# A DoRA linear layer on one core: the last three blocks loaded in 2 MB pieces behind two chunks of short rows, five chunks of short-row stores, earlier queued stores, and ScalarE for the first rounding

## The chip, the cores and the metric

One core of a Trainium2 chip. The metric is the device time of one execution in microseconds (us), median of several runs. Every timed run also carries the span that its own trace shows, about 1.3 us less than the time.

## The reference

The weights are small; the work is a product of 32768 rows by 256 with a 256 by 256 matrix. Input and output are 33.6 MB each.

```python
# x: (16, 2048, 256) float32; W: (256, 256); lora_A: (256, 16); lora_B: (16, 256); m: (256,)
W_adapted = W + scale * (lora_A @ lora_B)
W_norm = np.sqrt(np.sum(W_adapted ** 2, axis=0, keepdims=True) + 1e-8)
W_final = W_adapted / W_norm * m
y = x.reshape(-1, 256) @ W_final
```

## The kernel before

x is cut into 8 blocks of 4 MB. A block has 8 chunks of 512 KB; in SBUF a partition holds 32 rows of x per block, 32 KB that are also contiguous in HBM. Five blocks are held in SBUF at a time, so blocks 5 to 7 reuse the room of blocks 0 to 2, and can be loaded only once those are stored. y is written over x in the same buffer.

Two chunks make a pair. GpSimd (POOL) rounds a pair to bf16, TensorE turns it (transposes, two bf16 values at a time seen as one float32), VectorE copies it out of PSUM, TensorE multiplies it by w_final, ScalarE copies the two products from PSUM over x. Loads go through SyncE's queue, stores through ScalarE's.

```python
loads = [(0, 2), (2, 2), (4, CH - 4)] + units[1 : XBUFS - 1]      # (first chunk, chunks)
loads += [((XBUFS - 1) * CH, CH - 3)]
loads += [(XBUFS * CH - 3 + c, 1) for c in range(3)] + units[XBUFS:]
...
stores = [(b * CH, CH, 19 + b) for b in range(F - 1)]             # (first, chunks, issued after chunk)
stores += [(G - CH, CH // 2, 24), (G - CH // 2, CH // 2, 24)]
FIRST = len(stores)
stores += [(G + c, 1, G + 3) for c in range(4)]
stores += [(G + 4, CH - 4, 47)]
stores += [(b * CH, CH, max(47, (b + 1) * CH - 1)) for b in range(F + 1, NBLK - 1)]
stores += [(g0, cnt, g0 + cnt - 1) for g0, cnt in units[-2:]]
...
# POOL waits at pair 15 until the third store has landed (a rest of some 25 us)
if p == REST:
    nc.gpsimd.wait_ge(sem(f"store{HALF}"), 16)
```

The three one-chunk loads and the four one-chunk stores have rows of 4 KB per partition where a whole block has 32 KB.

## Time and profile before

| | before |
|---|---|
| median time, first three runs | 163.13 us (163.13 to 163.31) |
| span in the profile | 161.3 us |
| DMA engines: first packet to last packet | 2.0 to 160.8 us |
| PE, ACT, POOL, DVE busy | 61, 40, 39, 29% |
| mean rate | 418 GB/s |

The lines that matter most are shown in the prediction below. Two more, from the timeline of the kernel before near its start (columns: start us, length us, engine, line, operation, what it writes and reads, count): the products that make w_final, and the first transposes whose data come from block 1.

```profile
13.55 2.45 DVE L236 TENSOR_TENSOR w_final<-wam,rnorm 128x256 bf16<-128x256 f32 x2
...
27.09 1.04 PE L304 MATMUL xt_ps<-identity,xb 128*128 128x128 f32 x8
```

And this is the DMA view of the stretch from 160.0 to 163.5 us, beyond the point where 15 of the 16 engines are done (packets, MB, share of 16 engines):

```profile
q10 hardware_dynamic: 2, 0.02, 1.1%
```

One data packet of 16 KB and its completion packet: a single DMA engine works there, and the kernel waits for it.

### The profile page before, as it was taken

The page shows a single profiled execution, that of the slowest core. Times are in us where ns is not written, and L with a number is a line of the kernel's source. Part 1 is how long each engine was busy: PE and PEld are TensorE (multiplying, and loading weights), DVE is VectorE, ACT ScalarE, POOL GpSimd, SP SyncE. Part 2 cuts the span into 40 slices and gives each one's busy share as a digit, 9 for nine tenths or more (in the row PEclk, how much of TensorE's full clock was granted, in tenths as well). Part 3 has the DMA queues.
Part 4 walks back from the last instruction along what each step waited for, and adds up shares of the span by engine and source line. Part 5 has one row for each costly group of instructions (what it writes and reads, how often), then busy time and mean ns, then how long its engine had stood idle before and what let it go on. Part 6 is the DMA issues. An engine that isn't in the chain of part 4 may idle for free. (4 is left out here: it accounts for less than half of the span.)

```text
span 161.3 us, 2012 instructions
## 1 busy us (share of the span) xinstructions
PE 98.1 (61%) x786; PEld 85.6 (53%) x786; DVE 46.6 (29%) x44; ACT 64.1 (40%) x67; POOL 62.9 (39%) x39
## 2 busy tenths in 40 slices
PE   0490899999997920000799949999999980000000
PEld 0260789999996710000689937999799970000000
DVE  0539533535443500000224413445344500000000
ACT  3010068686776370000057643686767681000000
POOL 1174327868684000002938066497667400000000
PEclk9999999999999985555569995999999996555555
DMA  5999999999899999899999999999999999999994
GB/s 163 429 453 459 390 512 398 390 512 398 374 487 439 390 463 456 363 419 422 400 434 424 437 455 422 396 453 431 412 487 398 422 479 398 408 496 398 398 439 211
DMA packets 4357, 67.42 MB, mean 418 GB/s; under 512 B 626, under 2 KB 643, under 8 KB 1667
## 3 DMA queue, kind: packets, MB, share of 16 engines
q1 hardware_dynamic: 2160, 33.82, 49.2%
q10 hardware_dynamic: 2194, 33.59, 48.9%
q14 instruction: 3, 0.02, 0.0%
HBM read 33.85 MB, written 33.55 MB: 418 GB/s over the span
## 5 line engine op out<-in xcount | busy, mean ns | idle before, releaser
L258 ACT COPY x_sb<-y_ps 128x1024 f32<-128x1024 f32 x64 | 62.2, 1015 | 61.5 <-PE y_ps L318 60.2
L199 POOL CAST xb<-x_sb 128x2048 bf16<-128x2048 f32 x32 | 60.4, 1895 | 62.8 <-DMA out_dram<-x_sb 24.7
L318 PE MATMUL y_ps<-w_final,xt 128*128 128x256 bf16 x512 | 66.5, 286 | 2.5 <-PEq L293 2.5
L240 DVE COPY xt<-xt_ps 128x1024 f32<-128x1024 f32 x32 | 39.2, 1224 | 74.3 <-PE xt_ps L304 74.3
L318 PEld LDWEIGHTS y_ps<-w_final,xt 128*128 128x128 bf16 x512 | 52.3, 103 | 10.9 <-issue 3.2
L304 PE MATMUL xt_ps<-identity,xb 128*128 128x128 f32 x264 | 37.2, 288 | 25.7 <-PEq L293 25.7
L304 PEld LDWEIGHTS xt_ps<-identity,xb 128*128 128x128 f32 x264 | 32.3, 150 | 27.7 <-issue 27.2
L274 PE MATMUL y_ps<-identity,a_nat 128*16 128x128 f32 x2 | 0.6, 396 | 4.1 <-DMA a_nat<-in_lora_A_dram 4.1
L285 PE MATMUL y_ps<-sq,ones 128*128 128x256 f32 x4 | 2.1, 675 | 1.6 <-DVE sq L225 1.6
L250 ACT ACTIVATE norm<-y_ps,eps_col 128x256 f32<-128x256 f32 x1 | 0.5, 473 | 5.6 <-PE y_ps L285 5.6
L236 DVE TENSOR_TENSOR w_final<-wam,rnorm 128x256 bf16<-128x256 f32 x2 | 2.5, 1266 | 0.0
L285 PEld LDWEIGHTS y_ps<-sq,ones 128*128 128x128 f32 x4 | 1.2, 326 | 2.3 <-DVE sq L225 2.1
L274 PEld LDWEIGHTS y_ps<-identity,a_nat 128*16 128x16 f32 x2 | 0.1, 88 | 4.1 <-issue 4.1
L248 ACT ACT_TABLE_LOAD x1 | 1.3, 1283 | 2.4 <-issue 2.4
L205 POOL MEMSET xb<- 128x2048 bf16 x1 | 1.8, 1804 | 0.7 <-PE xt_ps L304 0.7
L233 DVE RECIPROCAL rnorm<-norm 128x256 f32<-128x256 f32 x1 | 1.7, 1747 | 0.0
L227 DVE COPY m_all<-y_ps 128x256 f32<-128x256 f32 x1 | 0.4, 424 | 3.3 <-PE y_ps L290 3.3
L290 PE MATMUL y_ps<-m_row,ones 1*128 1x256 f32 x2 | 1.2, 710 | 0.0
L216 DVE CAST b_bf<-b_nat 16x256 bf16<-16x256 f32 x1 | 0.3, 280 | 3.2 <-DMA b_nat<-in_lora_B_dram 3.2
L221 DVE SCALAR_TENSOR_TENSOR wa<-y_ps,w_nat 128x512 f32<-128x512 f32 x1 | 0.7, 692 | 0.8 <-PE y_ps L278 0.8
L278 PE MATMUL y_ps<-b_bf,aT 16*128 16x256 bf16 x2 | 0.6, 402 | 0.5 <-DVE aT L218 0.5
L290 PEld LDWEIGHTS y_ps<-m_row,ones 1*128 1x128 f32 x2 | 0.5, 308 | 0.7 <-issue 0.7
(13 smaller groups left out, 3.3 us busy)
## 6 DMA issues: line engine op xcount, KB each, us to landing
x_sb<-in_x_dram SPq DMA_DIRECT2D x5, 4096.0 KB, 28.7
out_dram<-x_sb ACTq DMA_DIRECT2D x5, 4096.0 KB, 20.9
out_dram<-x_sb ACTq DMA_DIRECT2D x5, 2048.0 KB, 26.7
x_sb<-in_x_dram SPq DMA_DIRECT2D x3, 2048.0 KB, 33.4
x_sb<-in_x_dram SPq DMA_DIRECT2D x1, 2560.0 KB, 44.7
x_sb<-in_x_dram SPq DMA_DIRECT2D x2, 1024.0 KB, 6.0
out_dram<-x_sb ACTq DMA_DIRECT2D x4, 512.0 KB, 43.8
x_sb<-in_x_dram SPq DMA_DIRECT2D x3, 512.0 KB, 19.5
```

Of the source, the lines that this page charges most:

```text
L199: nc.gpsimd.tensor_copy(out=xb_bufs[p % NXB][:], in_=x_bufs[b % XBUFS][:, 2 * c * J : 2 * (c + 1) * J, :],).then_inc(sem("rounded"), 1)
L205: nc.gpsimd.memset(xb_bufs[NPR % NXB][:], 0.0).then_inc(sem("rounded"), 1)
L221: nc.vector.scalar_tensor_tensor(out=wa[:], in0=ab_ps, scalar=float(scale), in1=w_nat[:], op0=ALU.mult, op1=ALU.add).then_inc(dv, 1)
L233: nc.vector.reciprocal(out=rnorm[:], in_=norm[:]).then_inc(dv, 1)
L236: i = nc.vector.tensor_mul(out=w_final[:, t], in0=wam[:, t], in1=rnorm[:])
L240: nc.vector.tensor_copy(out=xt_bufs[p % NXT][:].rearrange("p r t -> p (r t)").bitcast(FP32), in_=xt_ps[p % 2][:],).then_inc(sem("copied"), 1)
L248: nc.scalar.activation(out=warm[:], in_=eps_col[:], func=AF.Sqrt)
L258: nc.scalar.copy(out=x_bufs[b % XBUFS][:, c * J : (c + 1) * J, :], in_=y_ps[g % 2][:]).then_inc(sem("room"), 1)
L285: i = nc.tensor.matmul(n2_ps, ones[:], sq[:, t, :], start=(t == 0), stop=(t == KC - 1))
L290: nc.tensor.matmul(mb_ps, ones[0:1, :], m_row[:], start=True, stop=True).then_inc(pe, 1)
L304: i = nc.tensor.transpose(xt_ps[p % 2][:, j * P : (j + 1) * P], xb_bufs[p % NXB][:, j, :].bitcast(FP32), identity[:],)
L318: i = nc.tensor.matmul(y_ps[h][:, j, :], xt_bufs[p % NXT][:, r : r + P, t], w_final[:, t, :], start=(t == 0 and (j % (J // 2)) == 0), stop ...
```

## The change

The intent is to keep both queues fed with better proportions. As the prediction reads from the trace, the two queues take turns on a DMA engine, one packet each, and a packet is one row; so short rows hold one queue back without stopping it. The change makes only two chunks of loads short (not three), follows them at once by blocks 5 to 7 in halves with waits of their own, makes five chunks of stores short (not four), queues blocks 3 and 4 for storing from chunk 44 on, and shortens the start by having ScalarE round the first pair.

```diff
-    loads = [(0, 2), (2, 2), (4, CH - 4)] + units[1 : XBUFS - 1]
-    loads += [((XBUFS - 1) * CH, CH - 3)]
-    loads += [(XBUFS * CH - 3 + c, 1) for c in range(3)] + units[XBUFS:]
+    loads = [(0, 2, 2 * J), (2, 2, 2 * J), (4, 4, 4 * J)]         # third number: rows of x (1 KB each) in one packet
+    loads += [(b * CH, CH, CH * J) for b in range(1, XBUFS - 1)]
+    loads += [(H - CH, 6, 6 * J), (H - 2, 2, J)]
+    loads += [(g0, 4, 4 * J) for g0 in range(H, NCH, 4)]
-    stores += [(G - CH, CH // 2, 24), (G - CH // 2, CH // 2, 24)]
+    stores += [(G - CH, 3, 3 * J, G), (G - 5, 5, 5 * J, G)]
-    stores += [(G + c, 1, G + 3) for c in range(4)]
-    stores += [(G + 4, CH - 4, 47)]
-    stores += [(b * CH, CH, max(47, (b + 1) * CH - 1)) for b in range(F + 1, NBLK - 1)]
+    stores += [(G, 4, J, G + 3), (G + 4, 1, J, G + 4)]
+    stores += [(G + 5, CH - 5, (CH - 5) * J, 44), (G + CH, CH, CH * J, 44)]
+    stores += [(b * CH, CH, CH * J, (b + 1) * CH - 1) for b in range(F + 2, NBLK - 1)]
...
-        if loads[n][0] == XBUFS * CH:            # block 5: waits for stores 0, 1 and 2
+        if loads[n][0] == H + CH:                # block 6: waits for store 1
+            wait_store(nc.sync, 1)
+        if loads[n][0] == H + 2 * CH:            # block 7: waits for stores 2 and 3
...
-    for p in range(NPR):
+    for p in range(1, NPR):
...
+        if p == 1:
+            nc.gpsimd.wait_ge(sem("dve"), 6)
+        if p == 2:
+            nc.gpsimd.wait_ge(sem("dve"), 8)     # w_final is done
...
+    wait_load(nc.scalar, 0)
+    nc.scalar.copy(out=xb_bufs[0][:], in_=x_bufs[0][:, 0 : 2 * J, :]).then_inc(sem("early"), 1)
...
+    nc.tensor.wait_ge(sem("load_m"), 16)         # product with m before the norm's, no longer after
+    nc.tensor.matmul(mb_ps, ones[0:1, :], m_row[:], start=True, stop=True).then_inc(pe, 1)
```

More of the change, by code (lines that the diff above doesn't have):

```diff
@@ L51 @@
     REST = 15
-    IDLE = 8
     NXT = 2
@@ L103, with pieces @@
     units += [(NCH - CH, CH // 2), (NCH - CH // 2, CH // 2)]
-    loads = [(0, 2), (2, 2), (4, CH - 4)] + units[1 : XBUFS - 1]
-    loads += [((XBUFS - 1) * CH, CH - 3)]
-    loads += [(XBUFS * CH - 3 + c, 1) for c in range(3)] + units[XBUFS:]
-    load_of = {g: n for n, (g0, cnt) in enumerate(loads) for g in range(g0, g0 + cnt)}
     F = NBLK - XBUFS
     G = F * CH
-    stores = [(b * CH, CH, 19 + b) for b in range(F - 1)]
-    stores += [(G - CH, CH // 2, 24), (G - CH // 2, CH // 2, 24)]
-    FIRST = len(stores)
-    stores += [(G + c, 1, G + 3) for c in range(4)]
-    stores += [(G + 4, CH - 4, 47)]
-    stores += [(b * CH, CH, max(47, (b + 1) * CH - 1)) for b in range(F + 1, NBLK - 1)]
-    stores += [(g0, cnt, g0 + cnt - 1) for g0, cnt in units[-2:]]
-    HALF = FIRST - 2
+    H = XBUFS * CH
+    loads = [(0, 2, 2 * J), (2, 2, 2 * J), (4, 4, 4 * J)]
+    loads += [(b * CH, CH, CH * J) for b in range(1, XBUFS - 1)]
+    loads += [(H - CH, 6, 6 * J), (H - 2, 2, J)]
+    loads += [(g0, 4, 4 * J) for g0 in range(H, NCH, 4)]
+    load_of = {g: n for n, (g0, cnt, _) in enumerate(loads) for g in range(g0, g0 + cnt)}
+    stores = [(b * CH, CH, CH * J, 19 + b) for b in range(F - 1)]
+    stores += [(G - CH, 3, 3 * J, G), (G - 5, 5, 5 * J, G)]
+    FIRST = len(stores)
+    stores += [(G, 4, J, G + 3), (G + 4, 1, J, G + 4)]
+    stores += [(G + 5, CH - 5, (CH - 5) * J, 44), (G + CH, CH, CH * J, 44)]
+    stores += [(b * CH, CH, CH * J, (b + 1) * CH - 1) for b in range(F + 2, NBLK - 1)]
+    stores += [(g0, cnt, cnt * J, g0 + cnt - 1) for g0, cnt in units[-2:]]
+    def pieces(entry):
+        return 16 * (entry[1] * J // entry[2])
     late = [nc.alloc_semaphore(f"store{n}") for n in range(FIRST, len(stores))]
@@ L132, in sem, with transfer, wait_load, wait_store @@
         return sems[name]
-    def in_sbuf(g0, cnt):
+    def transfer(engine, name, entry, dram, store):
+        g0, cnt, rows = entry[:3]
         b, c = divmod(g0, CH)
-        return x_bufs[b % XBUFS][:, c * J : (c + cnt) * J, :]
-    def in_dram(dram, g0, cnt):
         (u0, ucnt), = [u for u in units if u[0] <= g0 < u[0] + u[1]]
         unit = dram[u0 * J * P : (u0 + ucnt) * J * P].rearrange("(p j) k -> p j k", p=P)
-        return unit[:, (g0 - u0) * J : (g0 - u0 + cnt) * J, :]
+        for r in range(0, cnt * J, rows):
+            here = x_bufs[b % XBUFS][:, c * J + r : c * J + r + rows, :]
+            there = unit[:, (g0 - u0) * J + r : (g0 - u0) * J + r + rows, :]
+            src, dst = (here, there) if store else (there, here)
+            engine.dma_start(out=dst, in_=src).then_inc(sem(name), 16)
     def load_x(n):
-        nc.sync.dma_start(
-            out=in_sbuf(*loads[n]), in_=in_dram(x_flat, *loads[n])
-        ).then_inc(sem(f"load{n}"), 16)
+        transfer(nc.sync, f"load{n}", loads[n], x_flat, False)
     def store_y(n):
-        nc.scalar.dma_start(
-            out=in_dram(out_flat, *stores[n][:2]), in_=in_sbuf(*stores[n][:2])
-        ).then_inc(sem(f"store{n}"), 16)
+        transfer(nc.scalar, f"store{n}", stores[n], out_flat, True)
+    def wait_load(engine, g):
+        engine.wait_ge(sem(f"load{load_of[g]}"), pieces(loads[load_of[g]]))
+    def wait_store(engine, n):
+        engine.wait_ge(sem(f"store{n}"), pieces(stores[n]))
     nc.sync.dma_start(
@@ L162 @@
     for n in range(len(loads)):
-        if loads[n][0] == XBUFS * CH - 3:
-            nc.sync.wait_ge(sem("store0"), 16)
-        if loads[n][0] == XBUFS * CH:
-            for k in range(HALF + 1):
-                nc.sync.wait_ge(sem(f"store{k}"), 16)
-        if loads[n] == units[-1]:
-            nc.sync.wait_ge(sem(f"store{HALF + 1}"), 16)
+        if loads[n][0] == H - 2:
+            wait_store(nc.sync, 0)
+        if loads[n][0] == H + CH:
+            wait_store(nc.sync, 1)
+        if loads[n][0] == H + 2 * CH:
+            wait_store(nc.sync, 2)
+            wait_store(nc.sync, 3)
         load_x(n)
@@ L185 @@
     ).then_inc(sem("ident"), 1)
-    for p in range(NPR):
+    for p in range(1, NPR):
         b, c = divmod(p, PRB)
         for g in (2 * p, 2 * p + 1):
-            if g == 0 or load_of[g - 1] != load_of[g]:
-                nc.gpsimd.wait_ge(sem(f"load{load_of[g]}"), 16)
-        if p == 0:
-            nc.gpsimd.wait_ge(sem("dve"), 4)
+            if g == 2 or load_of[g - 1] != load_of[g]:
+                wait_load(nc.gpsimd, g)
+        if p == 1:
+            nc.gpsimd.wait_ge(sem("dve"), 6)
+        if p == 2:
+            nc.gpsimd.wait_ge(sem("dve"), 8)
         if p == REST:
-            nc.gpsimd.wait_ge(sem(f"store{HALF}"), 16)
+            wait_store(nc.gpsimd, FIRST - 2)
         if p >= NXB:
@@ L205 @@
     nc.gpsimd.memset(xb_bufs[NPR % NXB][:], 0.0).then_inc(sem("rounded"), 1)
-    for _ in range(IDLE):
-        nc.gpsimd.wait_ge(sem("ident"), 1)
     dv = sem("dve")
@@ L225 @@
     nc.vector.tensor_mul(out=sq[:], in0=wa[:], in1=wa[:]).then_inc(dv, 1)
-    nc.vector.wait_ge(sem("pe"), 4)
+    nc.vector.wait_ge(sem("pe"), 3)
     nc.vector.tensor_copy(out=m_all[:], in_=mb_ps).then_inc(dv, 1)
@@ L237 @@
     i.then_inc(dv, 1)
+    nc.vector.wait_ge(dv, 8)
+    nc.vector.sem_inc(sem("room"), 2)
     for p in range(NPR):
@@ L243 @@
         ).then_inc(sem("copied"), 1)
+    for engine, idle in ((nc.gpsimd, 8), (nc.vector, 24)):
+        for _ in range(idle):
+            engine.wait_ge(sem("ident"), 1)
     nc.scalar.wait_ge(dv, 1)
     nc.scalar.activation(out=warm[:], in_=eps_col[:], func=AF.Sqrt)
-    nc.scalar.wait_ge(sem("pe"), 3)
+    wait_load(nc.scalar, 0)
+    nc.scalar.copy(out=xb_bufs[0][:], in_=x_bufs[0][:, 0 : 2 * J, :]).then_inc(
+        sem("early"), 1
+    )
+    nc.scalar.wait_ge(sem("pe"), 4)
     nc.scalar.activation(
@@ L260 @@
         ).then_inc(sem("room"), 1)
-        due = [n for n in range(len(stores)) if stores[n][2] == g]
+        due = [n for n in range(len(stores)) if stores[n][3] == g]
         if due:
@@ L288 @@
     i.then_inc(pe, 1)
-    nc.tensor.wait_ge(sem("load_m"), 16)
-    nc.tensor.matmul(mb_ps, ones[0:1, :], m_row[:], start=True, stop=True).then_inc(pe, 1)
     def take(name):
@@ L300, in turned @@
     def turned(p):
-        take("rounded")
         for j in range(2 * J):
@@ L325, in product @@
             i.then_inc(sem("product"), 1)
+    nc.tensor.wait_ge(sem("early"), 1)
     turned(0)
-    nc.tensor.wait_ge(dv, 8)
-    nc.tensor.sem_inc(sem("room"), 2)
     with nc.Fori(0, NPR // 2, 1, engines=[PE], head_slot={PE: 128}):
+        take("rounded")
         turned(1)
         product(0)
+        take("rounded")
         turned(0)
@@ L340 @@
     tc.compile()
-    for s in late:
-        nc.sync.wait_ge(s, 16)
+    for k, s in enumerate(late):
+        nc.sync.wait_ge(s, pieces(stores[FIRST + k]))
         nc.sync.sem_clear(s)
```

## The prediction

> **What bounds the kernel now.** I read the busy table by slices first, then the DMA queues, then the engine table by stage, then the timeline around each transfer. From slice 2 to slice 39 of the 40 the DMA engines are as good as full:
>
> ```profile
> DMA  5999999999899999899999999999999999999994
> GB/s 163 429 453 459 390 512 398 390 512 398 374 487 439 390 463 456 363 419 422 400 434 424 437 455 422 396 453 431 412 487 398 422 479 398 408 496 398 398 439 211
> ...
> q1 hardware_dynamic: 2160, 33.82, 49.2%
> q10 hardware_dynamic: 2194, 33.59, 48.9%
> ```
>
> q1 carries the loads and q10 the stores; together they hold the 16 engines for 98.1% of 161.3 us, which is 158.3 us. The first 2.0 us pass before the first packet. No compute engine is over 61% busy. The table of stages (columns: PE, weight loads, DVE, ACT, POOL, granted clock, DMA share, GB/s) says the same where it matters:
>
> ```profile
> 2.00:48.00 46.00, 37.64 (x282) 32.05 (x283) 21.95 (x22) 21.95 (x24) 26.08 (x14) 1.00 1.01 428
> 58.00:82.00 24.00, 4.82 (x26) 3.80 (x24) 1.22 (x1) 1.89 (x3) 5.62 (x3) 0.53 1.00 420
> 82.00:115.00 33.00, 30.40 (x256) 27.12 (x255) 12.68 (x11) 20.27 (x22) 19.11 (x11) 0.93 1.01 432
> 133.00:159.00 26.00, 0.00 (x0) 0.00 (x0) 0.00 (x0) 0.57 (x1) 0.00 (x0) 0.53 0.98 424
> ```
>
> In the last of these stages only the final half us of ACT is left and the stores run alone; the compute has a lead of some 26 us. In the timeline the last store is issued at 133.7 us and the tail is pure transfer:
>
> ```profile
> 46.79 0.37 ACTq L149 DMA_DIRECT2D out_dram<-x_sb  x1
> 58.89 23.24 SPq L144 DMA_DIRECT2D x_sb<-in_x_dram  x7
> 75.73 3.73 POOL L199 CAST xb<-x_sb 128x2048 bf16<-128x2048 f32 x2 [24.69 <-DMA out_dram<-x_sb]
> 112.23 1.38 ACTq L149 DMA_DIRECT2D out_dram<-x_sb  x3
> 133.68 0.34 ACTq L149 DMA_DIRECT2D out_dram<-x_sb  x1
> ```
>
> The 24.7 us wait of POOL is therefore not lost time: the transfers run through it at 420 GB/s. The end of the kernel is start-up plus the work of the busiest DMA engine.
>
> **What the cost of a packet is.** From the DMA view of single stretches (packets include one 4-byte completion packet per engine and transfer):
>
> ```profile
> q1 hardware_dynamic: 400, 12.06, 100.0%
> ...
> q1 hardware_dynamic: 112, 3.67, 84.9%
> q10 hardware_dynamic: 118, 0.42, 10.2%
> ...
> q10 hardware_dynamic: 79, 1.29, 100.9%
> ```
>
> The first line is 14 to 42 us: 368 packets of 32 KB fill 28 x 16 engine-us, 1.217 us each. The next two are 83 to 93 us: 102 packets of 4 KB take 16.3 engine-us, 0.159 us each. The last is 117 to 120 us: 79 packets of 16 KB, 0.613 us each. A line through these is 0.0376 us per KB plus some 0.008 us per packet. A packet is one partition's row of a transfer, so cutting rows shorter costs 8 ns per added row, no more.
>
> **What the Trainium skill says.** "DMA: Bandwidth & Descriptors", section "Queues, rings and completion order": each engine takes turns between its queues, one packet at a time. The trace agrees: from 83 to 93 us, 96 load packets of 32 KB went beside 102 store packets of 4 KB, one for one. That is the lever of this change: the row length sets a queue's share. The same page, section "Where 436 GB/s comes from", puts the ceiling of the ports at 435.2 GB/s; this trace has 431 GB/s where 32 KB rows run alone, so there is next to no rate left to win. "SBUF — State Buffer", section "Who interferes with whom": a VectorE instruction with two SBUF inputs waits for GpSimd where that reads SBUF. The two products that make w_final average 1266 ns beside a POOL cast here, against 0.38 us each for the equally large wam, so the trace agrees. "TensorE: Matmul & The Clock Gate", section "Part 1", has the clock at half after an idle window; the granted clock here is 0.53 from 58 to 82 us.
>
> **Part 1, the start.** ScalarE rounds chunks 0 and 1 instead of POOL, POOL stays out of VectorE's way until w_final is done, the product with m goes ahead of the norm. Now w_final is finished at 16.0 us and the first product starts at 18.4. After: norm near 10 us, reciprocal 1 to 1.7 us, w_final 0.8 us undisturbed, so near 12.5 us, and products from some 14 us. That is 3 to 4 us at the front, but pair 4 must wait for block 1, whose load lands at 23.0 us, then POOL rounds 1.9 us: the transposes of pair 4 go from 27.1 to 25.4 at best. From there a pair costs PE 2.62 us and loads 2.43, so 1.7 us of lead stay, and the first store is issued near 45 us instead of 46.8. At that time the DMA engines are busy with loads. Worth on the end: 0.
>
> **Part 2, the loads.** I replay both queues with the packet costs above, one packet each in turn, and two store packets already in flight when a load is issued. Before, this gives: store 1 ends 68.4, stores 2 and 3 at 74.6 and 80.8, short loads 82.1, the 4 MB loads 93.1 and 104.0, the last load 115.7; the trace has these all within 0.3 us, so I trust it. After: loads up to chunk 37 need to 49.5, and with store 0 the engines reach 59.2 (before 58.2, one chunk more is in). Two chunks in 4 KB rows (16 packets per engine) start near 64 and go with 4 packets of store 1, 8 of store 2 (12 KB), 4 of store 3 (20 KB): 69.5, 74.5, 78.2. Halves in 16 KB rows follow at once, already queued: first lands 86.8, then 93, 99, 105, 111, 118.7. Forty short store packets per engine (32 before) lie beside 16 KB rows, and then the 12 KB rows of chunks 29 to 31. Loads end 3 us later, with one chunk and most of three more already stored: the same bytes are moved.
>
> **Part 3, the stores.** Chunk 44 should be computed near 101 us, so blocks 3 and 4 are in the queue 17 us before they are needed; block 5 near 108, needed at 130; block 6 near 117, needed at 140. No gap. POOL waits for store 2 to about 75.5, as before. Block 5 arriving at 87 and not 93 removes the 5.2 us wait of POOL at 94 us and one cold-clock dip; compute ends near 131.5, before 133.6. Hidden as well.
>
> **Sum.** Rows per engine go from 224 to 240: 16 x 8 ns = +0.13 us; two more completion packets of 9 ns: +0.02. One more term comes from the trace's record of single packets: one engine ends at 160.8, the others at 159.3 to 159.8. It takes some 75 ns longer for each 32 KB store packet while compute runs beside stores (48 to 58, and 121 to 135 us), some 6%. Stores alone beside compute last 17 us before (115.6 to 132.7) and about 13 after, so 4 x 0.06 = -0.24. Total: 163.13 + 0.15 - 0.24 = **163.0 us**.
>
> **Rivals.** *A hole in the DMA queues.* If the load queue runs dry (chunks 48 on wait for store 1, chunks 56 on for stores 2 and 3) or PE comes too late for the stores, each us of hole is a us of time. For: nothing is held back by more than a few us around 84. Against: the replay has each wait met more than 10 us early. It would make 164 to 167. *The slow engine.* If its lag follows something else than compute, such as what lands on it, it may vanish (-1.2 us, 161.9) or double (164.3). *The earlier start is real.* If the lead of compute mattered, 1.7 us would come off, 161.4; the full DMA row of 2 to 159 us speaks against it. *More packets cost more than 8 ns* when short rows mix: store packets took up to 1.1 us instead of 0.61 around 79.9, 0.3 us on most engines; that may come or go.
>
> **Range and chances.** The terms are -0.24 and +0.15, the unknowns some 0.5 each, so 162.2 to 163.9. Faster by 2% means 159.9, below start-up plus 157.5 us of packets plus the 2.3 us from the last packet to the measured time: 2%. Slower by 2% means a 3.3 us hole: 3%.
>
> **What would show it.** DMA slices stay at 9, busy share of both queues sums to some 158.4 us, the w_final products fall to 0.4 us, the first store is issued near 45, POOL has no 5 us wait near 94, loads end near 118, and the last packet ends between 160 and 161.5. A slice of DMA at 7 or less in the middle, or a busiest engine that ends elsewhere by over 1 us, would prove me wrong.

## The result

| | before | after |
|---|---|---|
| median, 6 runs each | 163.22 us (162.66 to 163.65) | 162.87 us (162.57 to 163.29) |
| ratio, 95% interval | | 0.9981 (0.9956 to 1.0006) |
| second measurement, another chip | 162.93 us (11 runs) | 163.00 us (6 runs) |
| ratio, 95% interval | | 1.0010 (0.9978 to 1.0042) |
| span of the profiled run | 161.3 us | 161.3 us |

A ratio is the mean time of one kernel's fast runs over that of the other's in the same rounds, so it is not quite the ratio of the medians. The time stayed the same; both intervals hold 1.

The slices and the DMA queues of the kernel after, as they stand on its page (DMA busy in tenths, GB/s, then packets, MB, share of 16 engines for loads and stores):

```profile
DMA  4999999999999999989999999999999999999995
GB/s 167 425 457 455 390 512 398 390 512 398 423 390 480 398 463 426 431 365 453 423 403 444 407 437 427 422 423 430 443 483 398 423 473 408 406 480 415 386 443 219
...
q1 hardware_dynamic: 2304, 33.82, 49.2%
q10 hardware_dynamic: 2338, 33.59, 48.9%
```

There are 144 more packets in each queue, and the two shares are the same to the tenth. The stages (busy time of PE, weight loads, DVE, ACT and POOL with their counts, then the granted clock, which is the share of TensorE's full speed that it was given, DMA share, GB/s) are full as before:

```profile
2.00:48.00 46.00, 36.89 (x281) 31.90 (x282) 20.36 (x22) 23.66 (x25) 23.97 (x13) 0.96 1.01 431
58.00:82.00 24.00, 4.44 (x21) 3.61 (x22) 1.23 (x1) 1.74 (x2) 5.62 (x3) 0.53 1.01 430
82.00:118.00 36.00, 35.40 (x318) 32.59 (x317) 15.92 (x13) 25.27 (x27) 22.66 (x12) 0.98 1.01 426
131.00:159.00 28.00, 0.00 (x0) 0.00 (x0) 0.00 (x0) 0.04 (x1) 0.00 (x0) 0.57 1.00 428
```

The compute did become smoother: between 82 and 118 us PE is busy for 35.4 of 36 us. But at the end the stores again run alone for 28 us. The timeline, with the lines that answer to those of before:

```profile
11.88 0.76 DVE L241 TENSOR_TENSOR w_final<-wam,rnorm 128x256 bf16<-128x256 f32 x2
25.57 1.94 PE L321 MATMUL xt_ps<-identity,xb 128*128 128x128 f32 x8 [4.11 <-PEq L311]
27.30 2.67 PE L335 MATMUL y_ps<-w_final,xt 128*128 128x256 bf16 x16
46.89 0.37 ACTq L146 DMA_DIRECT2D out_dram<-x_sb  x1
75.52 3.73 POOL L208 CAST xb<-x_sb 128x2048 bf16<-128x2048 f32 x2 [24.38 <-DMA out_dram<-x_sb]
104.49 0.86 ACTq L146 DMA_DIRECT2D out_dram<-x_sb  x2
131.15 0.34 ACTq L146 DMA_DIRECT2D out_dram<-x_sb  x1
```

w_final is finished 3.4 us sooner (12.6 against 16.0), and yet the first store is issued at 46.89 us against 46.79. The second and third lines tell why. PE had to wait 4.1 us for block 1, and its clock fell; this is the stretch from 26 to 28 us (columns as for the stages, the granted clock is 0.50):

```profile
26.00:28.00 2.00, 2.00 (x12) 1.75 (x11) 0.46 (x1) 0.00 (x0) 1.69 (x2) 0.50 1.22 524
```

The same eight transposes took 1.94 us where they had taken 1.04, and the 16 products 2.67 us where a warm pair takes 1.91 (both from these timelines). That is 0.9 + 0.8 = 1.7 us, a little more than the lead of 1.5 us with which these transposes began (25.57 against 27.09). The last store is issued at 131.2 us against 133.7, which nobody waits for.

At the end of the kernel after, the DMA view from 160.0 to 163.5 us again has one data packet with completions:

```profile
q10 hardware_dynamic: 3, 0.02, 1.1%
```

### The profile page after: what moved, and what is told of

It reads as the page before. It is cut to its first block, busy times and chain, and to the rows that moved or that the text cites. A ratio compares the mean times of both kernels' runs of the same rounds, so it can differ in the third digit from the quotient of the medians.

```text
span 161.3 us, 2027 instructions
## 1 busy us (share of the span) xinstructions
PE 96.0 (60%) x786; PEld 84.8 (53%) x786; DVE 45.0 (28%) x44; ACT 66.0 (41%) x68; POOL 60.9 (38%) x38
## 5 line engine op out<-in xcount | busy, mean ns | idle before, releaser
L208 POOL CAST xb<-x_sb 128x2048 bf16<-128x2048 f32 x31 | 58.4, 1893 | 63.5 <-DMA x_sb<-in_x_dram 24.8
L335 PE MATMUL y_ps<-w_final,xt 128*128 128x256 bf16 x512 | 64.1, 279 | 3.9 <-PEq L311 3.8
L335 PEld LDWEIGHTS y_ps<-w_final,xt 128*128 128x128 bf16 x512 | 51.0, 100 | 11.5 <-issue 4.9
L321 PEld LDWEIGHTS xt_ps<-identity,xb 128*128 128x128 f32 x264 | 32.8, 151 | 26.4 <-issue 25.9
L264 ACT CAST xb<-x_sb 128x2048 bf16<-128x2048 f32 x1 | 1.9, 1898 | 2.6 <-DMA x_sb<-in_x_dram 2.6
L241 DVE TENSOR_TENSOR w_final<-wam,rnorm 128x256 bf16<-128x256 f32 x2 | 0.8, 422 | 0.0
```

The lines of the kernel that those rows point to most:

```text
L208: nc.gpsimd.tensor_copy(out=xb_bufs[p % NXB][:], in_=x_bufs[b % XBUFS][:, 2 * c * J : 2 * (c + 1) * J, :],).then_inc(sem("rounded"), 1)
L264: nc.scalar.copy(out=xb_bufs[0][:], in_=x_bufs[0][:, 0 : 2 * J, :]).then_inc(sem("early"), 1)
L321: i = nc.tensor.transpose(xt_ps[p % 2][:, j * P : (j + 1) * P], xb_bufs[p % NXB][:, j, :].bitcast(FP32), identity[:],)
L335: i = nc.tensor.matmul(y_ps[h][:, j, :], xt_bufs[p % NXT][:, r : r + P, t], w_final[:, t, :], start=(t == 0 and (j % (J // 2)) == 0), stop ...
```

## The experiments

One of the six runs of the last-store experiment was slow and is left out of its ratio. Packet times below that no view prints are read from the trace's own record of each DMA packet; a completion packet of 4 bytes ends each engine's part of a transfer, so it tells when each engine finished. The records don't name the engine of a packet; an engine is followed from one packet to the next, which starts 3 to 4 ns before the former's end.

### The parts of the change, one at a time

The start put back, new loads and stores kept:

```diff
-    for p in range(1, NPR):                     # ScalarE rounds pair 0 (its copy taken out)
+    for p in range(NPR):
-            nc.gpsimd.wait_ge(sem("dve"), 6)     # and 8 at pair 2
+            nc.gpsimd.wait_ge(sem("dve"), 4)     # at pair 0
```

> The changed kernel with its start put back as it was (POOL rounds the first pair, norm before the product with m), new loads and stores kept. Theory of full queues: the time is start-up plus the packets of the busiest DMA engine, so the start is worth nothing: 162.6 to 163.5 us, ratio to before 0.996 to 1.002, first store issued near 47 us and still before the loads end at 49.5. Rival, a lead of compute that counts while the new transfers cost as much: 164 to 165 us.

Measured: 162.72 us, ratio to before 0.9982 (0.9965 to 1.0000). From its timeline:

```profile
13.89 2.45 DVE L239 TENSOR_TENSOR w_final<-wam,rnorm 128x256 bf16<-128x256 f32 x2
...
46.88 0.37 ACTq L146 DMA_DIRECT2D out_dram<-x_sb  x1
```

The slow w_final is back (2.45 us, POOL rounds beside it), and the first store is issued at 46.88 us, within 0.01 us of the changed kernel. So the new start is worth nothing, not even as a lead of compute.

The opposite: the loads, stores and waits of before, with the new start.

```diff
-    loads += [(H - CH, 6, 6 * J), (H - 2, 2, J)]
-    loads += [(g0, 4, 4 * J) for g0 in range(H, NCH, 4)]
+    loads += [(H - CH, CH - 3)] + [(H - 3 + c, 1) for c in range(3)] + units[XBUFS:]
...                                               # stores and the waits of SyncE likewise
```

> The changed kernel with the loads, stores and their waits of before, new start kept. Full queues: same, 162.6 to 163.5 us; POOL has its wait of some 5 us for block 5 near 94 us again, and it costs nothing. Rival, the start is worth its 1.7 us and the new transfers lose them again: 161.2 to 161.8 us.

Measured: 163.25 us, ratio 1.0008 (0.9986 to 1.0031). POOL's wait for block 5 is there, in its timeline:

```profile
94.91 3.73 POOL L208 CAST xb<-x_sb 128x2048 bf16<-128x2048 f32 x2 [5.18 <-DMA x_sb<-in_x_dram]
```

5.2 us of waiting, no measurable cost. The two halves of the change, taken apart, are each the same as the whole within the intervals, and the rival with a hidden gain and an equal loss has no room left: it wanted 161.2 to 161.8 us here and 164 to 165 above.

### The changed kernel again

> The changed kernel once more, unedited, to see whether its 0.2% over the kernel before holds on another chip. The sum of the prediction (-0.24 +0.15 us) gives a ratio of 0.9995; the first measurement 0.9981. If the gain is real: 0.997 to 0.999 again. If it is scatter between runs: an interval that holds 1.

Measured: 163.00 us against 162.93, ratio 1.0010 (0.9978 to 1.0042). The 0.2% of the first measurement did not hold; it was scatter.

### What a row costs

Blocks 1 to 3, which are loaded while nothing is stored, in rows of 4 KB and not 32 KB.

```diff
-    loads += [(b * CH, CH, CH * J) for b in range(1, XBUFS - 1)]
+    loads += [(b * CH, CH, J) for b in range(1, XBUFS - 1)]
```

> Blocks 1 to 3 loaded in rows of 4 KB and not 32 KB, so 168 rows and 21 completion packets more per DMA engine, no other change. At 8.3 ns for a row and 9 ns for a completion packet: +1.4 +0.2 = +1.6 us, 164.2 to 164.8 us; block 3 lands some 1.6 us later. Rival, short rows cost much more than their packet overhead[...]: 5 us or more. Rival, a row costs nothing where nothing mixes: 162.9 us.

Measured: 163.92 us, ratio to before 1.0051 (1.0029 to 1.0073), so 1.1 us over the changed kernel's first median, and 1.5 us in the span. The range was missed by 0.3 us. In the DMA view from 14 to 42 us the load queue moved less in the same time:

```profile
q1 hardware_dynamic: 3156, 11.49, 102.7%
```

It is 11.49 MB where the kernel before had 12.06 MB (shown in the prediction). By the completion packets the three blocks took 1.5 us longer (the first engine had them in 30.65 us and not 29.14, the last one in 30.68 and not 29.15), which over 168 rows per engine is 9 ns for a row with its share of completions; 9.4 were expected. The span grew by the same 1.5 us, the median by 1.1; the difference is no larger than the scatter between runs. Short rows cost little more than their packets, and not nothing: both rivals fall.

### Transfers without compute

Wrong result: x is stored as it came. POOL, PE, VectorE and ScalarE's copies are taken out, and a store waits for the loads up to the chunk after which it was issued.

```diff
-        nc.scalar.wait_ge(sem("product"), g + 1)
-        nc.scalar.copy(...)
+        wait_load(nc.scalar, ...)                # the loads up to chunk g, the one it is issued after
```

> Wrong result on purpose: the same transfers with the same row lengths, but nothing computes; a store waits for the load of its last chunk instead. Full queues: the floor of the transfers, and 163 us less only what compute does to the DMA engines. If one engine falls behind only where compute runs beside 32 KB stores, then all 16 engines end within some 0.4 us of each other near 159.7 us and the time is 161.4 to 162.1 us. Rival, that engine is slow by itself: it still ends about 1 us after the others, 162.7 to 163.3 us. Rival, compute or its waits hold transfers up in the changed kernel: under 161 us.

Measured: 162.28 us (161.73 to 162.61), ratio to before 0.9959 (0.9941 to 0.9976); the profiled run was the fastest, 161.73. It is 0.2 us over the expected range in the median, and still the first theory's result: all 16 engines end between 159.7 and 160.0 us, where the changed kernel's end between 159.3 and 160.7, the last 0.7 us after the last but one. Its DMA view from 160.0 us on holds no data any more:

```profile
q10 hardware_dynamic: 1, 0.00, 0.0%
```

So the whole of compute, with all its waits, costs these transfers about 0.7 us, through one DMA engine: the other 15 end no later with compute than without, in the two profiled runs. One thing was not the same: with no compute to wait for, the first stores began among the loads of block 3, which landed at 49.0 us and not 42.1. With the loads done, from 121 us on, the first engine finishes each store within some 0.4 us of the changed kernel's. For these transfers, then, no arrangement of the compute can be expected to win more than about 0.7 us.

### A hole on purpose

All stores after chunk 28 held until chunk 60 is done.

```diff
-    stores += [(G + 5, CH - 5, (CH - 5) * J, 44), (G + CH, CH, CH * J, 44)]
-    stores += [(b * CH, CH, CH * J, (b + 1) * CH - 1) for b in range(F + 2, NBLK - 1)]
+    stores += [(G + 5, CH - 5, (CH - 5) * J, 60), (G + CH, CH, CH * J, 60)]
+    stores += [(b * CH, CH, CH * J, 60) for b in range(F + 2, NBLK - 1)]
...                                               # the last two stores: not before chunk 60 either
```

> All stores after chunk 28 held until chunk 60 is done. Loads then end near 117.0 us with the store queue empty; chunk 60 is done near 125.6 us and the first store packet follows 1.5 us later, so a hole of some 10 us near 117 to 127 us. Full queues: a hole costs its whole length, 172 to 174 us. Rival, the tail of stores has room to take it up (26 us in which nothing computes): 163 us.

Measured: 171.74 us (two runs, 171.70 and 171.79), just under the range. The stage from 116 to 127 us (columns as above):

```profile
116.00:127.00 11.00, 10.97 (x102) 9.98 (x99) 4.63 (x4) 6.79 (x7) 5.80 (x4) 1.00 0.11 45
```

PE is full and DMA is at 0.11, so 0.89 x 11 = 9.8 us are lost; the span grew by 9.1 (170.4 against 161.3). The 0.7 us between are the slow engine: here most of the compute fell into the hole, and the last engine ended at 170.0 us with the others at 169.4 to 169.6. A hole is paid in full, and the 26 us without compute at the end take up nothing of it.

### What slows one DMA engine

Four kernels give the tail, from 131 us on, something to do beside the stores.

```diff
+    with nc.Fori(0, 14, 1, engines=[PE], head_slot={PE: 128}):     # after the last product
+        for t in range(KC):
+            for j in range(8):
+                nc.tensor.matmul(xt_ps[0][:, (j % 4) * OUT : (j % 4 + 1) * OUT],
+                    xt_bufs[1][:, j * P : (j + 1) * P, t], w_final[:, t, :], start=True, stop=True)
```

> The changed kernel with 224 further matmuls on TensorE after the last product, some 24 us into the tail of stores, results unused. If compute on TensorE is what makes one DMA engine take some 75 ns longer for a 32 KB store packet (6%), that engine loses 1.2 to 1.5 us more and the time is 164.0 to 164.5 us. Rival, TensorE is not what does it: 162.6 to 163.3 us and the last engine ends about 1 us behind, as now.

Measured: 163.78 us, ratio to before 1.0059 (1.0029 to 1.0090), 0.2 us short of the range. In its timeline the additional matmuls fill most of the tail:

```profile
131.81 24.62 PE L358 MATMUL xt_ps<-w_final,xt 128*128 128x256 bf16 x224
```

The last engine ended at 161.8 us (160.7 without them).

```diff
+    for k in range(23):                                            # after the last store is issued
+        nc.scalar.copy(out=extra[:], in_=y_ps[0][:]).then_inc(sem("extra"), 1)
+        nc.scalar.wait_ge(sem("extra"), k + 1)
```

> The changed kernel with 23 further copies of 128x1024 from PSUM to a spare tile on ScalarE after the last store is issued, some 24 us into the tail. If ScalarE (its writes to SBUF, or the records of its instructions) slows that DMA engine: 164.0 to 164.5 us. Rival, it is not ScalarE: 162.6 to 163.3 us.

Measured: 162.95 us, ratio 1.0011 (0.9976 to 1.0047), and the last engine ended at 160.8 us. The time is that of the rival; but these were only 23 instructions, and the packet records below show how little so few can be expected to do.

```diff
-                nc.tensor.matmul(... w_final[:, t, :] ...)                                # 16 a turn, 256 columns
+                nc.tensor.matmul(... w_final[:].rearrange("p t o -> p (t o)") ...)        # 8 a turn, 512 columns
```

> As the kernel with further matmuls in the tail, but 112 of 512 columns and not 224 of 256: the same busy time of TensorE with half the instructions. The 224 made the last DMA engine end 1.1 us later in their profile. If what slows it goes by instructions (their fetch or their records): 0.5 to 0.6 us later, 163.2 to 163.5 us. If it goes by busy time (data read and written, power): 1.0 to 1.2 us later, 163.7 to 164.2 us.

Measured: 163.51 us, ratio 1.0031 (0.9988 to 1.0073). The times alone decide little, since that interval holds 1, and neither does the end of the last engine (161.8 us): all engines of this run were late by 0.4 us or more before the tail, and the last but one ended at 161.2.

A last kernel of this kind had waits on a semaphore that is already up instead of matmuls in the loop, so that nothing is computed and no data are read or written:

```diff
+    with nc.Fori(0, 14, 1, engines=[PE], head_slot={PE: 128}):
+        for _ in range(32):
+            nc.tensor.wait_ge(sem("ident"), 1)
```

> As before, but the further loop of TensorE holds 14 times 32 waits on a semaphore that is already up, and no matmul. By instructions alone: the last DMA engine still ends later than now, by up to 1 us as far as the loop lasts. By the work of the array: no change, 162.6 to 163.3 us.

Measured: 163.20 us in two runs (163.17 and 163.24), ratio to before 1.0017 (0.9965 to 1.0069), which lies in the range of no change but cannot exclude a delay of half a us. The timeline doesn't show waits; the view of their line does, and it says how long the loop lasted (PEldq is TensorE's sequencer; the trace has 224 waits where the program has 14 x 32; why only half is not known):

```profile
L357 PEldq EVENT_SEMAPHORE  x224: 51/51/51, 130.4 to 159.5; - x112
```

The packet records decide. For one and the same transfer, the 4 MB store that runs from about 141 to 151 us, the slow engine's 8 packets of 32 KB took

| in the tail | slow engine, us | over the others, us | instruction records, 141.4 to 151.0 us | ns for each |
|---|---|---|---|---|
| nothing (changed kernel) | 9.68 | 0 | 1 | |
| 224 matmuls of 256 columns | 10.14 | 0.46 | 188 | 2.4 |
| 112 matmuls of 512 columns, same busy time | 9.92 | 0.24 | 97 | 2.4 |
| waits on a semaphore, no matmul | 9.87 | 0.19 | 83 | 2.3 |
| 23 copies on ScalarE | 9.71 | 0.03 | 9 | about 3 |

(The fourth column counts all instructions that the trace has in that stretch, weight loads and the loop's own included.) Half the matmuls with the same busy time give half the delay, and waits that compute nothing give the same delay for each record. While the full compute runs, from 121.3 to 131.0 us of the changed kernel, the rate is again 0.51 us for 199 records, 2.5 ns each. So what slows this engine goes by the number of instructions, and neither by how long TensorE is busy nor by what it computes; most of them are TensorE's here, and nine of ScalarE's are too few to give a rate of their own. Loads don't show it: of the changed kernel's 368 load packets from 14 to 42 us, beside full compute, none took over 1.22 us. In the run with waits this engine ended at 161.2 us; another, which was late before the tail and took 9.68 us here, ended within 0.04 us of it.

What an instruction does to that engine is open. Every run here carries a span of its own, so a record of each instruction that is written out while the kernel runs is a possible cause, as are other things that come with every instruction. Fetching of instructions by DMA stands in the trace as a queue of its own, q14; it has no packet in that stretch in any of these runs. Without a run whose instructions are not recorded, nothing here tells whether an unrecorded kernel has this delay at all.

### Relieving the slow engine

The last 2 MB store cut by partitions.

```diff
+            if store and g0 == NCH - CH // 2:
+                for lo, hi in ((0, 112), (112, 120), (120, 128)):
+                    engine.dma_start(out=dst[lo:hi], in_=src[lo:hi]).then_inc(sem(name), 16)
+                continue
```

> The changed kernel with its last 2 MB store cut by partitions into 112, 8 and 8, so that (if such pieces go to the lowest-numbered engines) eight engines carry 9 rows of 16 KB and the other eight 7, each row 0.61 us. If the engine that ends last is one of the eight relieved: it ends 0.6 us earlier and the others 0.6 later, all near 160.1, and the time is 0.4 to 0.6 us under the changed kernel, 162.2 to 162.5 us. Rival, it is one of the eight that get more: 0.6 us or more over, 163.4 to 164.1 us. The profile also tells which half of the engines it is in.

Measured: 164.97 us for the five fast runs (163.46 to 165.40; the slow one 166.52), ratio 1.0090 (1.0037 to 1.0143). This failed, by more than its rival foresaw. The engine that ended last completed three pieces at the end (at 162.1, 162.7 and 163.3 us), so it carried 9 rows: it is one of the eight that got more. Beyond that, eleven data packets of 16 KB took 0.74 to 1.30 us where they take 0.61 elsewhere, at a time when several engines wrote out of the same few partitions; that this is the cause is not shown. So no version here beats both kernels.

## Why the prediction was right

Time: 163.0 us, in 162.2 to 163.9; measured were 162.87 and 163.00.

**The bound** was read rightly. The DMA engines are full from 2 to 159 us in both kernels, the two queues' shares are the same to a tenth of a percent, and the kernel without compute is only 0.7 us faster than the kernel before. The hole on purpose shows what the reading rests on: it cost 9.1 us for 9.8 us of emptiness.

**The replay of the queues** held nearly everywhere. Predicted and found, as the first engine finished each: loads up to chunk 37, 49.5 and 49.5; store 1, 69.5 and 69.5; store 2, 74.5 and 74.4; short loads, 78.2 and 77.5; the first half of block 5, 86.8 and 86.8; end of the loads, 118.7 and 118.2 us. Alternation of the two queues packet by packet is enough to foresee them.

**Part 1** was worth 0, as said, but a step of its working was wrong: "From there a pair costs PE 2.62 us and loads 2.43, so 1.7 us of lead stay, and the first store is issued near 45 us instead of 46.8". It was issued at 46.89. The step left out that the earlier PE would wait longer for block 1 (4.1 us) and resume at a low clock (0.50), although the same case stood in the profile of before, at 96 us. The lead was 1.5 us when pair 4 began, near the 1.7 foreseen, and the cold pair took all of it back.

**Parts 2 and 3** were hidden, as said. Chunk 44 was done at 104.4 us and not 101, and still long before the stores of blocks 3 and 4 were due; the wait at 94 us went, and putting it back cost nothing.

**The sum** had its main term about right. "Stores alone beside compute last 17 us before (115.6 to 132.7) and about 13 after, so 4 x 0.06 = -0.24": from the end of the loads on, the slow engine's store packets took together 1.12 us more than their size takes on the other engines in the kernel before (eight of 16 KB 0.28, twelve of 32 KB 0.85) and 0.80 us in the changed one (six of 12 KB 0.12, ten of 32 KB 0.68). So the term measured -0.32. But its picture, that the loss goes with the time that compute runs beside stores, was only half of it: it goes with the instructions executed meanwhile, as the tail experiments show. The other term, +0.15 for rows, lies under the 0.2 us by which the packets' total moves between runs for other reasons (158.3 us for each engine before, 158.1 after, 158.4 with the old start). The last engine ended at 160.8 before and 160.7 after, 161.1 when the changed kernel ran again. That the sum of -0.09 fits the first two is luck at the level of 0.1 us.

**The rivals.** There was no hole and no gain by the start. The slow engine was there in both kernels; that it follows the instructions is shown, as it vanishes without compute and grows in the tail with more matmuls, and with waits alone. The stretched store packets around 79.9 us appear again in the changed kernel near 78 and 82 us (20 KB packets took 0.79 us on average and not 0.76), and not without compute, where all took 0.76.

## What to carry to other kernels

When the DMA row is full from the first packet to the last, count what the transfers themselves cost (bytes, rows, completions, start) before reordering compute: here a 5 us wait of POOL and 3.4 us of earlier start were both worth nothing. What can still go wrong in such a kernel is a hole, which costs its whole length. An engine that runs ahead of its data may come to rest, resume at a lower clock and give its lead back. Before a small delay is put down to what an engine computes, try the same number of instructions that compute nothing.

## What the Trainium skill lacked or had wrong

- "SBUF — State Buffer", section "SBUF: two separate sides", says "A DMA cannot be slowed by a compute op, and vice versa." The runs don't show it wrong for SBUF, since waits that touch no data slowed a DMA engine as well, but a reader of traces will meet an exception for which no page has a number: while instructions ran, one DMA engine took longer for its store packets, by about 2.4 ns for each recorded instruction (estimate from 0.46 us for 188, 0.24 us for 97 and 0.19 us for 83 records). With the full compute that was some 60 to 75 ns on a 1213 ns packet of 32 KB, and a kernel with such transfers and no compute was 0.4% faster than the kernel before (ratio 0.9959). The recording of instructions is not ruled out as the cause.
- "DMA: Bandwidth & Descriptors", section "Why small descriptors are slow (HBM only)", has a fixed cost for a packet in cycles, but no measured cost of a shorter row for loads of several KB from SyncE. Here a fit to packets of 4, 16 and 32 KB gives 8 ns, and cutting 32 KB rows into 4 KB ones cost 9 ns for each added row with its completions.
